# A fourth ring buffer and a third set of gated activations in the loop over expert_v

## The chip, the core and the metric

The kernel runs on one core of one Trainium2 chip, in one launch. The metric is the device time of a whole execution in microseconds (us), median of several runs. Before the change it is 3137.03 us, the median of three runs that took from 3127.26 to 3152.71 us.

## The reference, cut to what matters

The program computes two transformer blocks on 512 tokens of 1024 features in float32. The change touches the end of the second block alone, a feed-forward layer of 16384 experts, each a row `u_e` of `expert_u` and a row `v_e` of `expert_v`:

```python
expert_idx, gates = ...      # 8 heads x 16 experts of every token, with softmax gates
u = jnp.take(expert_u, ib, axis=0)
act = jax.nn.gelu(jnp.einsum('td,thkd->thk', xb, u))
w = gb * act
v = jnp.take(expert_v, ib, axis=0)
out = jnp.einsum('thk,thkd->td', w, v)
```

The layer's output is added to its input, and a last normalisation follows.

## The kernel before

**Tokens.** The 512 tokens are four tiles of 128. For three of them (the dense tiles, `NDENSE = 3`) the kernel computes every expert and multiplies by a gate matrix that is zero for experts not chosen. The fourth tile gathers the 128 chosen rows of each token: 128 indirect DMAs from `expert_u` (here `eu`) and then 128 from `expert_v` (`ev`), each of 128 rows of 1024 floats (512 KB), into a ring of four buffers `urow` (L1323). VectorE works on each gathered tile with one operation: L1332 for `eu` (a product with the token's row, summed), L1342 for `ev` (added to `po`). The gathers are issued by GpSimd (L1324).

**Exact products.** TensorE multiplies in three passes (`mm3`, L261): every operand is split into a high part `hi` and the rest `lo`. A weight tile is 128 x 1024 floats, 512 KB. `_load` (L227) brings it into one of three `raw` buffers by a DMA on SP's queue; `_split` (L232) makes `hi` on ScalarE (L238) and `lo = raw - hi` (L241) on VectorE where the tile's running number is even, on GpSimd where it is odd. `hi` and `lo` have three buffers each. `next_w` (L247), called when tile i is about to be used, sees to it that tiles up to i+2 are split and tiles up to i+4 are being loaded.

**The stage of the change.** `peer` (L1416) first computes 40 of the 128 blocks of activations (`expert_act`, products with `expert_u`, tile name `ut` in DMAs), and the gate matrix, which goes to DRAM (`gd`). Then comes a loop over 128 blocks j of `expert_v` (L1444). Each iteration
- reads, every fourth time, gates of four blocks back (`gread`, two buffers of 768 KB, L1447, on SP's queue);
- gates the activations (`expert_gate`, L1395): `wf` on VectorE (L1400), `wh` on ScalarE (L1403), `wl` on VectorE (L1404), two buffers of each;
- multiplies them by the tile of `expert_v` (`expert_out`, L1407): 18 matmuls of 512 columns into the banks A, B, C and D;
- while j + 40 < 128, computes the activations of block j + 40: 24 matmuls of 384 columns into the bank `acc`;
- issues the gathers of the fourth tile that are due, 2 * 256 / 210 = 2.44 of them in an iteration that also has activations, 1.22 in one that has not (L1469).

In this loop tiles of `ev` and `ut` alternate in the ring for the first 88 iterations; the `ut` tiles are even (`lo` on VectorE), the `ev` tiles odd (`lo` on GpSimd). In the last 40 iterations only `ev` tiles are left and the two engines take turns.

**Order.** Every engine, and SP's queue, works through its instructions in one fixed order. A planner writes that order when the program is built, from the order in which the source names the operations, its own estimate of durations, and the buffers that it believes free; splits are given priority. What is late on the chip holds up everything behind it on the same engine. Each gather is also ordered behind the last GpSimd split that the source has named before it (L1326).

Of the kernel before, what the change touches and what calls it, by code (L numbers as in the profile page):

```python
# [23 lines left out]
# ---------------------------------------------------------------- host layout  # L24
def fm_tiles(w, cols=None):
    """[K, N] -> one [128, (K/128)*128] block per 128 output columns, split into ring tiles of 1024."""
    w = w if cols is None else w[:, cols]
    k, n = w.shape
    a = w.reshape(k // 128, 128, n // 128, 128).transpose(2, 1, 0, 3)
    return a.reshape(n // 128, 128, k // 1024, 1024).transpose(0, 2, 1, 3).reshape(-1, 128, 1024)  # L30


def tm_tiles(w):
    """[K, N] -> ring tiles of [128, 2 k-chunks, 512 columns], column blocks outermost."""
    k, n = w.shape
    a = w.reshape(k // 256, 2, 128, n // 512, 512).transpose(3, 0, 2, 1, 4)
    return a.reshape(-1, 128, 1024)


def fmvec(v):  # L40
# [4 lines left out]
NDENSE = 3      # token tiles whose experts are all computed; the last tile gathers its experts' rows  # L45
NFIFO = 40
IN_ORDER = ((0, 0), (0, 1), (0, 2), (0, 3), (1, 0), (1, 1), (1, 2), (1, 3))      # projections: mixer, heads
ONEHOT = "DDPDDDPP"     # engine of the second one-hot, by quartet of a block
NEARLY, NLATE, NLAG = 25, 3, 10      # products with expert_u before and after the gate matrix
# [3 lines left out]
    [x for n in range(8) for x in [(1, n), (0, n + GATE_AHEAD)] if x[1] < 8]    # gate a, branch; block  # L53
ATTN_STEP = 2
ELEM_AT = 2
FB = "acc; A m fpt; B fs; C pe fpo0; D fpo1"      # banks of the mixers' products
# [33 lines left out]
def prep(inp):  # L90
    """Lays the inputs out; every array is a permutation, slice or stack of inputs, or depends on shapes alone."""
# [77 lines left out]
# ---------------------------------------------------------------- program  # L169
class Prog:  # L170
    def __init__(self, tc, es, I, dbg=None):
        self.tc, self.nc, self.I, self.dbg = tc, tc.nc, I, dbg or {}
        nc = self.nc
        pool = lambda n, b, **k: es.enter_context(tc.tile_pool(name=n, bufs=b, **k))
        self.cp = pool("const", 1)
        self.tp = pool("tiny", 1)
        self.rp = pool("ring", 1)
        self.R = {}
        self.queue = []
        self.qi = 0  # L180
        self.loaded = []
        self.split_done = []
        self.pool_split = None

    # storage: every name of a tile stands for a tag with its number of buffers in the pool of the phase
    def open(self, es, name, spec, right=True, psum=False):
        """spec: "tag buffers name name ...; ..." """
# [9 lines left out]
    def banks(self, spec):  # L197
        """spec: "bank name name; ..." """
# [24 lines left out]
    # ring of weight tiles  # L223
    def want(self, aps):
        self.queue.extend(aps)

    def _load(self):  # L227
        raw = self.rp.tile([128, 1024], F32, tag="raw", name="raw", bufs=3)
        self.nc.sync.dma_start(raw, self.queue[len(self.loaded)])
        self.loaded.append(raw)  # L230

    def _split(self):  # L232
        i = len(self.split_done)
        raw = self.loaded[i]
        hi = self.rp.tile([128, 1024], F32R, tag="hi", name="hi", bufs=3)
        lo = self.rp.tile([128, 1024], F32R, tag="lo", name="lo", bufs=3)
# [10 lines left out]
    def next_w(self):  # L247
        i = self.qi
        self.qi += 1
        while len(self.split_done) < min(i + 3, len(self.queue)):  # L250
# [3 lines left out]
        while len(self.loaded) < min(i + 5, len(self.queue)):  # L254
# [5 lines left out]
    # products  # L260
    def mm3(self, out, a, b, start, stop):  # L261
        """out += a^T b with a, b given as exact (hi, lo) parts"""
# [5 lines left out]
    def gemm_fm(self, X, M=128, bank="acc", parts=1):  # L268
        """one block of 128 output features x 512 tokens; X: list of (hi, lo) FM chunks"""
# [12 lines left out]
    def gemm_tm(self, X, banks=("A", "A", "B", "B"), done=None, tail=2, head=1, ps=None, stop=True, hold=0):  # L282
        """512 output columns x 4 token tiles; the tiles end one after the other,
        the end of a tile behind the norm of the one `hold` before it"""
# [27 lines left out]
    def split(self, src, name):  # L312
        """FM f32 chunk in SBUF -> exact parts"""
# [8 lines left out]
    # constants  # L322
    def consts(self):
# [13 lines left out]
        # derived per-channel vectors  # L337
# [13 lines left out]
        # lower bound: softmax over the two rows, first row  # L351
# [8 lines left out]
        # f = lb + (1 - lb) (tanh / 2 + 1/2) = tanh * c1 + c0  # L360
# [7 lines left out]
    def attn_consts(self):  # L368
        """constants of the first mixers only"""
# [18 lines left out]
    def first_loads(self):  # L388
        """tokens, the first gain and the first weights in the order of their use"""
# [29 lines left out]
    def rstd_of(self, ss, n, eps, w=1):  # L419
        """(ss / n + eps) ** -0.5 of a small tile"""  # L420
# [7 lines left out]
    def new_U(self):  # L428
        """8 FM chunks of exact parts"""
# [4 lines left out]
    def rstd_row(self, ss):  # L434
        """(sum + eps) ** -0.5 of the two scaled square sums of a row"""
# [6 lines left out]
    def square(self, x, ss):  # L442
        """sum of squares / D along the row"""
# [3 lines left out]
    def norm_tile(self, i, gb, banks=("C", "D"), ss=None):  # L447
        """rmsnorm of one token tile of self.X, into its columns of the FM chunks; ss: with its first square sum"""
# [24 lines left out]
    def norm_fm(self, gb):  # L473
        """rmsnorm of self.X as 8 FM chunks of exact parts"""
# [6 lines left out]
    def tm_norm(self, X, gp, gn, early=None):  # L481
        """self.X += rmsnorm(X^T w) * gp, and the FM chunks of rmsnorm(self.X) * gn;
        early: the two halves of the product begun with the first chunks"""
# [35 lines left out]
    # ------------------------------------------------------------ block 1  # L519
# [10 lines left out]
    def lat_part(self, U):  # L530
# [19 lines left out]
        # forget gates of the attention heads: rows 32..39  # L550
# [18 lines left out]
    def fox_proj(self, c, U):  # L569
        """queries, keys and values of two heads"""  # L570
# [84 lines left out]
    def rwkv_elem(self, c):  # L655
        """two heads of the RWKV group on 128 channels"""
# [5 lines left out]
        # decay  # L662
# [15 lines left out]
        # in-context rate  # L678
# [9 lines left out]
        # normalised key  # L688
# [16 lines left out]
        # gate and bonus  # L705
# [15 lines left out]
    def rwkv_group(self, c, g_, e):  # L721
        """operands of four chunks: with Z = [state; values] of a head and U = (I - N)^-1 A0^T Z,
        y = A1^T Z + B1^T U and the next state is D^T Z + Bu^T U"""
# [8 lines left out]
        ar = self.b("AR", [128, 4, 2, 2, 64])         # chunk, A0 or A1, head, token  # L732
        bk = self.b("BK", [128, 4, 4, 64])
        m1 = self.b("M1", [128, 4, 2, 2, 64])         # chunk, head, y or state
        gm = self.b("GM", [128, 4, 2, 64])            # chunk, B1 or Bu
# [11 lines left out]
        # [b k] scaled to the end of their chunk, tokens on partitions  # L747
# [9 lines left out]
        # rows: even head (b; k), odd head: transposed from (k; b)  # L757
# [4 lines left out]
        # scores  # L762
# [18 lines left out]
        # values, tokens on partitions  # L781
# [9 lines left out]
    def rwkv_inv(self, e, g_, h):  # L791
        """(I - N)^-1 of two chunks by doubling"""
# [36 lines left out]
    def rwkv_fold(self, e, g_):  # L829
        """y and the next state as products with Z alone: [A1 D] + A0 ((I - N)^-1)^T [B1 Bu]"""  # L830
# [15 lines left out]
    def rwkv_scan(self, c, g_, e):  # L846
        """chunks in sequence"""
# [20 lines left out]
        # normalise per head, then features on partitions  # L868
# [44 lines left out]
    # ------------------------------------------------------------ block 2  # L913
    def column_sum(self, bank, a, names=("R", "sq")):
        """sums over the partitions, on all of them"""
# [9 lines left out]
    def head_scale(self, sq, n):  # L925
        """(mean square + eps) ** -0.5 of one head on all partitions; sq: sum of n blocks of squares"""
# [16 lines left out]
    def hgrn_in(self, h, U):  # L943
        """forget gate, key and query of one head"""
# [25 lines left out]
    def hgrn(self, h, a, sg):  # L970
# [14 lines left out]
        # the diagonal: sums over the channels, on all partitions  # L985
# [5 lines left out]
        while n <= 256:  # L991
            if n == 64:
                # the earlier tokens of a block by its later ones
# [59 lines left out]
    def gate_hg(self, U):  # L1053
        """sigmoid(gate_a) * (o_hg @ w_branch_hg), doubled"""
# [23 lines left out]
    def ret(self, h, U):  # L1078
# [19 lines left out]
        # scores, keys on partitions: the columns of the later queries  # L1098
# [56 lines left out]
    def merge(self, U):  # L1155
        """M = (sigmoid(gate_a) y_hg + sigmoid(gate_b) y_ret), m1 holds the doubled first term"""
# [31 lines left out]
    def add_out(self, M, gn):  # L1188
        """self.X += M^T w, and the FM chunks of rmsnorm(self.X) * gn"""
# [17 lines left out]
    def row_of(self, i):  # L1207
        """normalised tokens of tile i, tokens on partitions"""
# [23 lines left out]
    def retrieve(self, H4):  # L1232
        """top 16 sub-keys of every (head, half), then the top 16 of the pairs of every head"""
# [8 lines left out]
        for hp in range(4):  # L1242
# [4 lines left out]
            for c in range(4):  # L1247
# [10 lines left out]
                if c % 2:  # L1258
                    # both lists descend: pair (a, b) can only be chosen if (a + 1) (b + 1) <= 16,
                    # which b < 16 for a < 4 and b < 4 for the others contain  # L1260
# [13 lines left out]
    def decode(self, i, hp, ti, bs, bc):  # L1274
        """sub-key numbers (i, j) and gates of two heads of a token tile, slots (head, k) along the free dimension"""
# [34 lines left out]
    def gather_rows(self, i, row):  # L1310
        """experts of one token tile by their rows"""
# [33 lines left out]
    def slots_T(self, i):  # L1345
        """[slot, (i, j, gate), token] of one token tile"""
# [9 lines left out]
    def gate_matrix(self, slT, gd):  # L1356
        """gates[i, j, token] of the dense tokens into DRAM, 32 tokens at a time"""
# [25 lines left out]
    def expert_act(self, H4, j):  # L1383
        """gelu(u . h) of the 128 experts (., j) for the dense tokens"""
# [10 lines left out]
    def expert_gate(self, j, a, gr):  # L1395
        """gated activations of the 128 experts (., j), exact parts"""
        nc = self.nc
        n = NDENSE * 128
        wf = self.C([128, n], "wf", 2)
        nc.vector.tensor_tensor(wf.rearrange("p (b t) -> p b t", t=32), a.rearrange("p (b t) -> p b t", t=32),  # L1400
                                gr[:, :, j % 4, :], op=ALU.mult)
        wh, wl = self.C([128, n], "wh", 2, F32R), self.C([128, n], "wl", 2, F32R)
# [4 lines left out]
    def expert_out(self, ops, acc, i):  # L1407
        """token tile i += its gated activations times their rows of expert_v"""
# [7 lines left out]
    def peer(self, H4, gd, xd, row, out):  # L1416
# [24 lines left out]
        self.open_v()  # L1441
        acc = [[self.b(n) for n in ns] for ns in ("AA", "BB", "CD")]
# [38 lines left out]
    def final(self, i, y, gb, out):  # L1481
        """rmsnorm(self.X + y) of a token tile"""
# [15 lines left out]
def step(gen, n):  # L1498
    """n steps of a generator"""
# [7 lines left out]
def run_all(gens):  # L1507
    """interleave generators round-robin"""
# [9 lines left out]
def body(tc, I, out, dbg=None, manual=False):  # L1518
    nc = tc.nc
    with ExitStack() as es:  # L1520
# [20 lines left out]
        with ExitStack() as e1:  # L1541
# [22 lines left out]
            with ExitStack() as e2:  # L1564
# [3 lines left out]
                def prepare(u):  # L1568
                    """operands of the u-th group of four chunks"""
# [101 lines left out]
```

## Time and profile before

| | |
|---|---|
| median of three runs | 3137.03 us (3127.26 to 3152.71) |
| profiled execution, span from first to last instruction | 3129.2 us (the page gives no other time of it) |
| TensorE busy (matmuls) | 2961.4 us, 95% |
| VectorE, ScalarE, GpSimd busy | 62%, 39%, 48% |
| mean granted TensorE clock | 0.983 |
| the loop over `expert_v`, first matmul to last | 2182.3 to 3121.0 us |

Times below are in microseconds from the span's start. PE is TensorE, DVE is VectorE, ACT is ScalarE, POOL is GpSimd, SPq is SP's queue; PEld is the loading of weights into TensorE. A row such as `lo<-raw,hi` names the tile written and the tiles read. A bracket at the end of a row tells how long the engine had been idle before it and what ended that.

### The profile page before, as it was taken

The numbers are of one execution on the slowest core, as the hardware profiler recorded it, in microseconds if no ns is written. First come the engines' busy times: TensorE is split into PE (matmuls) and PEld (weight loads), VectorE is DVE, ScalarE is ACT, GpSimd is POOL, SyncE is SP. The second block draws the span as 40 slices with busy tenths as digits, with TensorE's granted clock in tenths as the row PEclk, the third lists the DMA queues.
The fourth block names the chain that finished last, engine by engine and source line by source line (L and its number), as shares of the span: only waits on it lengthen the run. The fifth ranks groups of instructions, "written<-read, shape, count | busy, mean of one in ns | idle before, by whom it ended". The sixth has DMA issues, their size and how long they took to land.

```text
span 3129.2 us, 40869 instructions
## 1 busy us (share of the span) xinstructions
PE 2961.4 (95%) x15129; PEld 2547.7 (81%) x15129; DVE 1938.7 (62%) x3421; ACT 1228.4 (39%) x1925; POOL 1508.5 (48%) x1150
## 2 busy tenths in 40 slices
PE   7999898999999999999999978888999999999998
PEld 6877787888878878888888868887888888888876
DVE  4247755443135653555423899997777777787788
ACT  5455644222243433444423324565333333333333
POOL 3222213222245652333323457866767677667665
PEclk9998999999999999999999989999999999999999
DMA  4120013333332213222333223446888988888886
GB/s 156 56 68 8 1 38 109 97 98 97 95 113 69 62 47 101 85 85 85 90 116 123 92 68 95 142 169 219 297 275 293 308 289 298 299 280 299 285 310 240
DMA packets 174359, 473.65 MB, mean 151 GB/s; under 512 B 15056, under 2 KB 64592, under 8 KB 172624
## 3 DMA queue, kind: packets, MB, share of 16 engines
q1 hardware_dynamic: 137296, 336.80, 33.8%
q0 software_dynamic: 36864, 134.23, 12.2%
q8 instruction: 120, 1.97, 0.3%
q14 instruction: 79, 0.65, 0.1%
HBM read 439.49 MB, written 31.46 MB: 151 GB/s over the span
## 4 chain that ended last, share of the span: by engine, by line
PE 69%; DVE 15%; DMA 7%; issue 5%; ACT 2%; POOL 1%; SPq 0%; DVEq 0%; POOLq 0%; ACTq 0%
PE acc L266 13%; PE acc L265 13%; PE acc L264 13%; DMA urow<-ev,ei 3%; PE A L266 3%; PE A L264 3%; PE A L265 3%; PE B L266 3%; PE B L265 3%; PE B L264 3%; DMA urow<-eu,ei 2%; PE pg L1377 2%; DVE lo L241 2%; PE i L804 1%; PE lev L981 1%
## 5 line engine op out<-in xcount | busy, mean ns | idle before, releaser
L241 POOL TENSOR_TENSOR lo<-raw,hi 128x1024 fp32r<-128x1024 f32 x278 | 689.6, 2481 | 912.9 <-ACT hi L238 875.8
L238 ACT ACTIVATE hi<-raw 128x1024 fp32r<-128x1024 f32 x501 | 529.3, 1057 | 1065.7 <-PE acc L265 441.4
L266 PE MATMUL acc<-u,lo 128*128 128x512 f32 (+3 forms) x2344 | 864.6, 369 | 39.2 <-DVE lo L241 21.2
L264 PE MATMUL acc<-u,hi 128*128 128x512 f32 (+3 forms) x2344 | 862.4, 369 | 15.0 <-ACT x L1392 6.3
L265 PE MATMUL acc<-u,hi 128*128 128x512 f32 (+3 forms) x2344 | 862.1, 368 | 0.7 <-DVE u L471 0.7
L266 PEld LDWEIGHTS acc<-u,lo 128*128 128x128 f32 (+1 forms) x2344 | 448.1, 191 | 96.2 <-DVE lo L241 27.6
L264 PEld LDWEIGHTS acc<-u,hi 128*128 128x128 f32 (+1 forms) x2344 | 447.8, 191 | 70.0 <-ACT eact L1392 6.7
L265 PEld LDWEIGHTS acc<-u,hi 128*128 128x128 f32 (+1 forms) x2344 | 448.3, 191 | 54.8 <-issue 2.7
L241 DVE TENSOR_TENSOR lo<-raw,hi 128x1024 fp32r<-128x1024 f32 x223 | 304.4, 1365 | 301.1 <-ACT hi L238 299.9
L1332 DVE SCALAR_TENSOR_TENSOR urow<-urow,h4row 128x1024 f32<-128x1024 f32 x128 | 201.5, 1595 | 109.2 <-DMA urow<-eu,ei 108.9
L1342 DVE SCALAR_TENSOR_TENSOR po<-urow,act,po 128x1024 f32<-128x1024 f32 x127 | 203.2, 1600 | 84.9 <-DMA urow<-ev,ei 83.5
L1324 POOL DMA_INDIRECT urow<-eu,ei x128 | 193.5, 1512 | 32.6 <-issue 19.0
L1324 POOL DMA_INDIRECT urow<-ev,ei x128 | 176.6, 1380 | 37.8 <-issue 18.2
L1403 ACT ACTIVATE wh<-wf 128x384 fp32r<-128x384 f32 x128 | 67.1, 525 | 272.3 <-PE D L265 243.5
L1368 DVE TENSOR_SCALAR ohA<-iota,slT 128x128 f32<-128x128 f32 x384 | 129.8, 404 | 0.9 <-PE pg L1377 0.7
L1377 PE MATMUL pg<-ohB,ohA 128*128 128x128 f32 x768 | 106.3, 280 | 25.0 <-DVE ohB L1374 12.5
L1377 PEld LDWEIGHTS pg<-ohB,ohA 128*128 128x128 f32 x768 | 97.4, 191 | 32.7 <-ACT gstage L1379 16.1
L1379 ACT ACTIVATE gstage<-pg 128x512 f32<-128x512 f32 x96 | 99.5, 1089 | 57.8 <-PE pg L1377 57.7
L1372 POOL TENSOR_SCALAR ohB<-iota,slT 128x128 f32<-128x128 f32 x144 | 98.2, 698 | 39.9 <-PE pg L1377 39.7
L266 PE MATMUL A<-hi,wl 128*128 128x512 f32 x256 | 95.8, 399 | 10.0 <-DVE wl L1404 9.9
L265 PE MATMUL A<-lo,wh 128*128 128x512 f32 x256 | 101.0, 395 | 0.8 <-POOL lo L241 0.8
L264 PE MATMUL A<-hi,wh 128*128 128x512 f32 x256 | 99.8, 390 | 0.6 <-ACT wh L1403 0.6
(539 smaller groups left out, 5395.9 us busy)
## 6 DMA issues: line engine op xcount, KB each, us to landing
raw<-ut SPq DMA_DIRECT2D x128, 512.0 KB
raw<-ev SPq DMA_DIRECT2D x128, 512.0 KB
raw<-w_ret SPq DMA_DIRECT2D x48, 512.0 KB
gd<-gstage SPq DMA_DIRECT2D x12, 2048.0 KB
gread<-gd SPq DMA_DIRECT2D x32, 768.0 KB
raw<-w_gu SPq DMA_DIRECT2D x44, 512.0 KB
raw<-w_hg SPq DMA_DIRECT2D x32, 512.0 KB
raw<-w_in SPq DMA_DIRECT2D x27, 512.0 KB
```

The source lines that it names most:

```text
L238: self.nc.scalar.activation(hi, raw, AF.Copy)
L241: r = eng.tensor_tensor(lo, raw, hi.bitcast(F32), op=ALU.subtract)
L264: mm(out, a[0], b[0], start=start, stop=False)
L265: mm(out, a[0], b[1], start=False, stop=False)
L266: return mm(out, a[1], b[0], start=False, stop=stop).ins
L1324: r = nc.gpsimd.indirect_dma_start(out=u, out_offset=None, in_=src, in_offset=bass.IndirectOffsetOnAxis(ap=ei[:, s:s + 1], axis=0))
L1332: nc.vector.scalar_tensor_tensor(u, u, 1.0, row, op0=ALU.mult, op1=ALU.mult, accum_out=act[:, s:s + 1])
L1342: nc.vector.scalar_tensor_tensor(o, u, act[:, s:s + 1], o, op0=ALU.mult, op1=ALU.add)
L1368: nc.vector.tensor_scalar(A4[:, r], self.iota, sl[:, 0, k + r:k + r + 1], sl[:, 2, k + r:k + r + 1], op0=ALU.is_equal, op1=ALU.mult)
L1372: nc.gpsimd.tensor_scalar(B4[:, r], self.iota, sl[:, 1, k + r:k + r + 1], None, op0=ALU.is_equal)
L1377: last = nc.tensor.matmul(p[:, r, :], A4[:, r], B4[:, r], start=True, stop=True)
L1379: nc.scalar.activation(st[:, :, q * 4:q * 4 + 4].rearrange("p j t -> p t j"), p, AF.Copy)
```

## The change

After the loop's pool has been opened, a flag `ext` is set to 1. From there on tiles whose running number is 3 modulo 4 take their `raw`, `hi` and `lo` from three extra buffers in the loop's pool, so that the ring has four places in place of three; `next_w` splits up to tile i+3 and loads up to tile i+6. `wf`, `wh` and `wl` get three buffers in place of two. No operation is added or taken out. The rest of the diff takes out comments and docstrings.

```diff
@@ __init__
         self.split_done = []
+        self.ext = 0
@@ ring of weight tiles
+    def ring(self, i, name, dt=F32):
+
+        if self.ext and i % 4 == 3:
+            return self.C([128, 1024], name + "x", 1, dt)
+        return self.rp.tile([128, 1024], dt, tag=name, name=name, bufs=3)
+
     def _load(self):
-        raw = self.rp.tile([128, 1024], F32, tag="raw", name="raw", bufs=3)
-        self.nc.sync.dma_start(raw, self.queue[len(self.loaded)])
+        i = len(self.loaded)
+        raw = self.ring(i, "raw")
+        self.nc.sync.dma_start(raw, self.queue[i])
         self.loaded.append(raw)
@@ _split
-        hi = self.rp.tile([128, 1024], F32R, tag="hi", name="hi", bufs=3)
-        lo = self.rp.tile([128, 1024], F32R, tag="lo", name="lo", bufs=3)
+        hi, lo = self.ring(i, "hi", F32R), self.ring(i, "lo", F32R)
@@ next_w
-        while len(self.split_done) < min(i + 3, len(self.queue)):
+        while len(self.split_done) < min(i + 3 + self.ext, len(self.queue)):
...
-        while len(self.loaded) < min(i + 5, len(self.queue)):
+        while len(self.loaded) < min(i + 5 + 2 * self.ext, len(self.queue)):
@@ expert_gate
-        wf = self.C([128, n], "wf", 2)
+        wf = self.C([128, n], "wf", 3)
...
-        wh, wl = self.C([128, n], "wh", 2, F32R), self.C([128, n], "wl", 2, F32R)
+        wh, wl = self.C([128, n], "wh", 3, F32R), self.C([128, n], "wl", 3, F32R)
@@ peer
         self.open_v()
+        self.ext = 1
```

## Rows read from the trace of the kernel before

**Rows 1.** Stretches: length, busy of PE, PEld, DVE, ACT, POOL; clock, DMA share, GB/s.
```profile
2182.20:2941.00 758.80, 737.44 (x3672) 665.75 (x3673) 571.71 (x609) 255.73 (x353) 536.30 (x301) 0.99 0.87 292
2941.00:3121.00 180.00, 168.88 (x722) 135.16 (x720) 153.66 (x151) 62.16 (x91) 110.26 (x63) 0.99 0.83 283
```
**Rows 2.** Timeline of TensorE: start, duration. Ends of the two stretches, one iteration between.
```profile
2182.26 0.50 PE L264 MATMUL A<-hi,wh 128*128 128x512 f32 x1 [0.31 <-ACT wh L1403]
...
2336.20 0.39 PE L264 MATMUL A<-hi,wh 128*128 128x512 f32 x1
...
2340.32 0.33 PE L264 MATMUL acc<-u,hi 128*128 128x384 f32 x1
...
2344.51 0.39 PE L264 MATMUL A<-hi,wh 128*128 128x512 f32 x1
...
2941.07 0.39 PE L264 MATMUL A<-hi,wh 128*128 128x512 f32 x1
...
3120.62 0.39 PE L266 MATMUL D<-hi,wl 128*128 128x512 f32 x1
```
**Rows 3.** Groups of TensorE's instructions from 2182.2 to 2941.0: count, busy, mean ns.
```profile
L266 PE MATMUL acc<-u,lo 128*128 128x384 f32 x696 | 238.0, 342 | 21.3 <-DVE lo L241 21.2
```
**Rows 4.** TensorE's waits from 2182.2 to 2941.0: total us, times, longest.
```profile
PE acc L266 <- DVE lo L241: 21.2, 19, 4.2
```
**Rows 5.** TensorE's waits from 2941 to 3121.
```profile
PE A L266 <- DVE wl L1404: 9.9, 7, 4.2
```
**Rows 6.** A short stretch (columns of rows 1) with the clock at half.
```profile
2312.00:2318.00 6.00, 4.79 (x15) 4.79 (x16) 5.97 (x10) 0.00 (x0) 3.34 (x3) 0.50 0.79 218
```
**Rows 7.** Timelines of three engines around one short wait of TensorE.
```profile
2349.03 1.05 ACT L238 ACTIVATE hi<-raw 128x1024 fp32r<-128x1024 f32 x1
...
2352.23 1.23 DVE L1332 SCALAR_TENSOR_TENSOR urow<-urow,h4row 128x1024 f32<-128x1024 f32 x1 [1.31 <-DMA urow<-eu,ei]
...
2354.44 3.43 DVE L241 TENSOR_TENSOR lo<-raw,hi 128x1024 fp32r<-128x1024 f32 x1
...
2357.92 0.44 PE L266 MATMUL acc<-u,lo 128*128 128x384 f32 x1 [0.48 <-DVE lo L241]
```
**Rows 8.** VectorE's waits from 2200 to 2930 (columns of rows 4).
```profile
DVE urow L1332 <- DMA urow<-eu,ei: 105.6, 59, 3.7
```
**Rows 9.** Tile urow from 2180 to 3110: ns min/median/max, first and last start; landing.
```profile
L1324 POOL DMA_INDIRECT urow<-eu,ei x128: 937/1682/2007, 2181.4 to 2632.4; - x128
...
L1342 DVE SCALAR_TENSOR_TENSOR po<-urow,act,po x127: 1271/1285/3370, 2646.5 to 3103.9; 128x1024 f32<-128x1024 f32 x127
...
DMA to landing us min/median/max: 4.2/6.5/9.6
```
**Rows 10.** Timelines of VectorE and GpSimd in the last stretch.
```profile
2984.17 4.03 POOL L241 TENSOR_TENSOR lo<-raw,hi 128x1024 fp32r<-128x1024 f32 x1 [1.63 <-ACT hi L238]
...
2985.97 2.64 DVE L1400 TENSOR_TENSOR wf<-eact,gread 128x384 f32<-128x384 f32 x1
2988.53 2.59 DVE L1342 SCALAR_TENSOR_TENSOR po<-urow,act,po 128x1024 f32<-128x1024 f32 x2
...
2989.74 0.95 POOL L1324 DMA_INDIRECT urow<-ev,ei  x1 [0.30 <-issue]
```
**Rows 11.** Durations of splits and gating in the whole loop (columns of rows 9).
```profile
L241 DVE TENSOR_TENSOR lo<-raw,hi x107: 1208/1219/3426, 2184.1 to 3112.3; 128x1024 fp32r<-128x1024 f32 x107
L241 POOL TENSOR_TENSOR lo<-raw,hi x106: 2352/2407/4253, 2188.1 to 3105.7; 128x1024 fp32r<-128x1024 f32 x106
...
L1400 DVE TENSOR_TENSOR wf<-eact,gread x96: 546/558/3155, 2236.1 to 3078.2; 128x384 f32<-128x384 f32 x96
```
**Rows 12.** Waits of ScalarE and of SP's queue in the loop.
```profile
ACT wh L1403 <- PE D L265: 243.5, 100, 4.1
...
SPq L1447 <- DVE wf L1400: 117.5, 29, 8.4
```
**Rows 13.** A short stretch (columns of rows 1) with DMA engines full.
```profile
2834.00:2838.00 4.00, 4.00 (x21) 3.49 (x21) 2.21 (x3) 1.44 (x2) 0.34 (x1) 1.00 0.99 352
```

## The prediction

> **What bounds the kernel now.** I read the loop over `expert_v` alone, because nothing outside it changes: first the busy time by stretch, then TensorE's timeline and its waits, then the engines that it waits for.
>
> By stretch [rows 1], TensorE is busy 737.4 of 758.8 us in the 88 iterations that also compute activations, and 168.9 of 180.0 in the last 40. The timeline gives the price of an undisturbed tile [rows 2]: the matmuls of a tile of `expert_v` start at 2336.20, those of the next `expert_u` tile at 2340.32, the next `expert_v` tile at 2344.51. So 4.12 us and 4.19 us, together 8.31 us. The first stretch, 2182.26 to 2941.07, holds 87 `expert_u` tiles (696 low-part matmuls, 8 a tile [rows 3]) and so 88 of `expert_v`: 88 x 4.12 + 87 x 4.19 = 727.1 us. It takes 758.8, an excess of 31.7 us. The last stretch should take 40 x 4.12 = 164.8 and takes 179.9 (to 3121.0, the last start plus 0.39): an excess of 15.1 us. **The change can return 46.8 us at most**, 1.5% of the kernel; no tile gets cheaper by it.
>
> The excess of the first stretch has a name: 19 waits for VectorE's `lo`, 21.2 us, the longest 4.2 [rows 4]. Behind the longest the granted clock stands at 0.50 of full speed, the 1.2 GHz level, in all of the 6 us shown [rows 6]: TensorE had stood idle before it fell. Such stretches, and gaps too small for the waits view, make up the other 10.5 us. One ordinary wait shows how it comes about [rows 7]: `hi` of the tile starts at 2349.03 and takes 1.05, so that `lo` could start at 2350.1. But VectorE stands in its fixed order before gathered rows that have not landed (1.31 us idle just before 2352.23), and starts `lo` at 2354.44; TensorE needed it 0.48 us before it came. In that stretch VectorE waits 105.6 us for gathers of `expert_u` alone [rows 8].
>
> **The change, part by part.** Nothing is added to or removed from any engine's work: the same loads, splits, gatings, gathers and matmuls. What moves is how early a tile may be split and loaded.
>
> *The fourth hi and lo.* In steady state `hi` of tile i+2 waits until tile i-1 has left its buffers; now it is tile i+3 that takes that place. The split starts at the same moment as before and is needed one tile later, 4.12 to 4.19 us. Every wait in rows 4 is at most 4.2 us, so one tile of margin covers each taken singly. They return only if lateness carries over from one iteration to the next. VectorE's room against that: 571.7 us busy in 758.8 [rows 1], 6.5 us of an iteration's 8.31, and most of its idle time is waiting for gathers, which passes when it runs late, since the rows have then landed. I take 28 of the 31.7 us (all but about a tenth), bounds 0 (order and lateness move along with the tile) and 31.7.
>
> *The fourth raw.* A load is issued when the place frees, so the same number of bytes goes out, with one tile more in flight. SP's queue is fixed too: loads stand behind `gread`, which waited 117.5 us in 29 times for the last `wf` of its buffer [rows 12]; a load held there now has a tile more before its split is late. Queue time added: none. DMA at full TensorE pace: an iteration moves two tiles of 512 KB, a quarter of 768 KB and 2.44 gathers of 512 KB, 2464 KB or 2.52 MB, in 8.31 us: 304 GB/s against 292 now at a share of 0.87 [rows 1]. In the last 40 it is 512 + 192 + 624 KB, 1.36 MB in 4.12 us: 330. A short stretch with the DMA engines full moved 352 [rows 13]. So the first stretch fits and the last one barely; cost 0 in the first, included below in the last.
>
> *The third gating set.* ScalarE stood 243.5 us before `wh` until TensorE had released the older set [rows 12], with the next `hi` queued behind it. That wait moves back by a tile; next in line there is the ring's own release, so alone it gives little in the first stretch. In the last it aims at the 9.9 us for `wl` [rows 5], where TensorE's waits lie.
>
> *The last 40.* What is late next is visible there. While GpSimd's `lo` ran, VectorE's `wf` took 2.64 us instead of 0.56 and GpSimd's `lo` 4.03 instead of 2.41 [rows 10, 11]: the two take turns. One tile then needs 1.22 x 1.285 for rows [rows 9], about 0.56 each for `wf` and `wl`, half of 1.22 and half of 2.41 for `lo` [rows 11]: 1.57 + 1.12 + 0.61 + 1.20 = 4.50 us. Consecutive rows of VectorE overlap a little (the `wf` of rows 10 ends at 2988.61, 0.08 us after the next operation started), and 3.7 such ends a tile bring it to 4.2. That is no less than TensorE's 4.12, and the stretch now goes at 179.9 / 40 = 4.50. A ring does not shorten this turn-taking, it only fills its gaps. I take 5 of the 15.1 us, bounds 0 and 15.1, nearer the lower, since the engine pair already needs the tile's time.
>
> The Trainium skill (SBUF — State Buffer, the box on VectorE blocking DMA) says more: while VectorE runs an operation that takes both port pairs, GpSimd cannot write the descriptors of its own DMAs. If the row sums were of that kind, the gathers' issue would join the turn-taking, 1.22 x 0.95 us a tile or more, and the last stretch could return nothing: a sum of 28. The rows do not bear that out: an issue of 0.95 us, among the shortest, ran inside a pair of unstretched `po` operations [rows 9, 10].
>
> *Start of the loop.* The new buffers lie in the loop's pool, so the first use may wait for memory of the gate phase. Tiles already loaded keep their old `raw`; the first `wf` waits for that phase anyway. I take 0, bounds 0 and 4 us (one tile).
>
> **The sum.** 28 + 5 = 33 us. The profiled span is 3129.2; it would become 3096. The median of the runs is 7.8 above that span, so I set the sum against the median: 3137 - 33 = **3104 us**, -1.05%.
>
> **Rivals.** *The whole excess goes* (chance 0.08): the pair of engines closes its gaps too, 3137 - 46.8 = 3090. For it: the waits for `wl` are exactly what the third set is for. Against: the 4.2 us above.
>
> *The wait moves along* (0.22): the planner puts each split just as far back in VectorE's order as it now has margin, or bandwidth at 304 GB/s makes the gathers land later, and half or less of the first stretch comes back: gain 0 to 17, time 3120 to 3137, middle 3128. For it: splits here run at planned places and VectorE does wait on gathers all along. Against: splits have priority, and nothing is put between.
>
> *Gathers become the bound* (0.12), the case on the slower side. The ring `urow` keeps four buffers. A gather holds one for about 1.7 us of issue, 6.5 of flight and 1.2 of VectorE, 9.4; four gathers come every 4 x (2632.4 - 2181.4) / 127 = 14.2 us [rows 9], so 4.8 us are free. A gather is ordered behind the last split GpSimd was given before it in the source; that split is now of a tile further ahead, which can hold the issue by up to a tile, 4.15 us, and one more 512 KB load in flight takes 1.8 us at 292 GB/s. Together 5.95, that is 1.1 over the free time; from 4.8 on each us over costs 256 / 4 = 64 us, so up to 3137 + 70 = 3207, and 3172 at half the overrun. Against: the ordering shifts the phase rather than the rate, and the longest landing, 9.6, is 3.1 above the median.
>
> That the change doesn't act is unlikely, since the numbers modulo 4 rotate through four places; if the planner loaded no earlier, the time stays 3137 (in the second rival).
>
> **How the numbers follow.** About 1% (31 us) is what a measurement of this kernel tells from no change. The forecast's own case has 0.58: 3095 to 3115, so a little over half of it lies below 3105.7. Faster: 0.33 + 0.08 + 0.02 = 0.43. Same: 0.25 + 0.20 = 0.45. Slower: 0.12. The range runs from 3086 (full excess, with a few us for the runs' spread) to 3140, which takes in the second rival and leaves out most of the third.
>
> **What would show it.** Right: in the first stretch the waits for `lo` fall below about 3 us, no half-clock stretch is left, an iteration takes 8.31 nearly throughout, and DMA rises to about 304 GB/s; the last 40 still take near 4.4 us each with the pair of engines full. Wrong: waits for `lo` of the same count and size at other places; TensorE waiting for `raw`; gathers landing well over 6.5 us, with GpSimd waiting for `urow`; or a last stretch near 165 us, which would refute the turn-taking bound.

## The result, and the profile after

The changed kernel takes **3087.99 us**, the median of four runs (3084.94 to 3091.29), against 3135.9 for the kernel before, run beside it (3127.26 to 3152.71). The ratio is 0.986, 95% interval 0.9829 to 0.9892. That is 48 us less; the forecast was 33 less and 3104 us, the range 3086 to 3140.

The profiled executions differ by 45.2 us in span, 3129.2 to 3084.0. Busy time of the two stretches of the loop after, with the columns of [rows 1]:

```profile
2177.00:2905.60 728.60, 728.60 (x3684) 663.12 (x3683) 570.02 (x607) 258.09 (x353) 535.70 (x300) 1.00 0.88 304
2905.60:3076.00 170.40, 165.31 (x722) 134.56 (x720) 159.39 (x152) 60.62 (x89) 110.77 (x65) 1.00 0.84 300
```

TensorE is busy all of the first stretch, the clock is granted whole, and the DMA engines move the 304 GB/s that the forecast asked of them, at a share of 0.88. VectorE and GpSimd do the same work as before, 570.0 and 535.7 us busy against 571.7 and 536.3, in 30 us less. TensorE's timeline, start and duration, at the bounds of the stretches (they answer to [rows 2]):

```profile
2177.41 0.39 PE L271 MATMUL A<-hi,wh 128*128 128x512 f32 x1
...
2905.66 0.39 PE L271 MATMUL A<-hi,wh 128*128 128x512 f32 x1
...
3075.43 0.39 PE L273 MATMUL D<-hi,wl 128*128 128x512 f32 x1
```

The first stretch takes 728.25 us in place of 758.8, within 1.2 us of the 727.1 reckoned for undisturbed tiles. The last takes 170.2 (to 3075.8) in place of 179.9. So the loop returns 30.6 + 9.8 = 40.4 us. The other 4.85 us lie ahead of it: the loop begins at 2177.41 in place of 2182.26, although the instructions stand in the same order in both programs up to some 8 us ahead of the loop. I take that part for drift between two executions: with only the gating sets changed, the kernel before began its loop at 2178.2.

TensorE's waits in the loop after (engine, line, what it waited for: total us, times, longest), one row where [rows 4, 5] had waits of 21.2 and 9.9:

```profile
PE A L273 <- DVE wl L1411: 4.9, 6, 1.9
```

The 19 waits for VectorE's `lo` are gone, with the half-clock stretches behind them. What has not gone is VectorE's waiting for gathered rows (from 2190 to 2905, the same columns), beside [rows 8]:

```profile
DVE urow L1339 <- DMA urow<-eu,ei: 91.5, 56, 5.0
DVE po L1349 <- DMA urow<-ev,ei: 56.2, 36, 4.8
```

By the median the gathers land no sooner (tile `urow`, min/median/max, beside the last row of [rows 9]):

```profile
DMA to landing us min/median/max: 2.0/7.0/10.8
```

VectorE still stands before late rows, up to 5.0 us at a time. TensorE no longer notices. The margin shows why. From the end of a `lo` on VectorE to the first matmul that reads it, the trace of before has a median of 3.6 us, and for 21 of the 87 `expert_u` tiles under 0.3. After the change the median is 7.4 us and the shortest 1.9: nearly one tile's time more. The planner's order of VectorE changed as well (every `lo` of the first stretch stood right behind a `wf`, now 25 of 85 do); what that does apart from the margin was not tried.

### The profile page after: what moved, and what is told of

It reads as the page before. It is cut to its first block, busy times and chain, and to the rows that moved or that the text cites. A ratio compares the mean times of both kernels' runs of the same rounds, so it can differ in the third digit from the quotient of the medians.

```text
span 3084.0 us, 40810 instructions
## 1 busy us (share of the span) xinstructions
PE 2945.5 (96%) x15129; PEld 2542.2 (82%) x15129; DVE 1940.8 (63%) x3421; ACT 1229.7 (40%) x1925; POOL 1507.6 (49%) x1150
## 4 chain that ended last, share of the span: by engine, by line
PE 77%; DVE 13%; issue 4%; DMA 2%; ACT 2%; POOL 2%; SPq 0%; DVEq 0%; POOLq 0%; ACTq 0%
PE acc L272 14%; PE acc L271 14%; PE acc L273 14%; PE A L273 3%; PE A L272 3%; PE A L271 3%; PE B L272 3%; PE B L271 3%; PE B L273 3%; PE pg L1384 2%; DMA urow<-ev,ei 2%; PE i L811 2%; PE lev L988 1%; DVE wk L1235 1%; PE C L273 1%
## 5 line engine op out<-in xcount | busy, mean ns | idle before, releaser
L248 POOL TENSOR_TENSOR lo<-raw,hi 128x1024 fp32r<-128x1024 f32 x224 | 553.0, 2470 | 758.2 <-ACT hi L245 729.1
L245 ACT ACTIVATE hi<-raw 128x1024 fp32r<-128x1024 f32 x447 | 472.5, 1057 | 944.2 <-PE acc L272 496.2
L248 DVE TENSOR_TENSOR lo<-raw,hi 128x1024 fp32r<-128x1024 f32 x223 | 318.2, 1427 | 297.3 <-ACT hi L245 297.0
L1349 DVE SCALAR_TENSOR_TENSOR po<-urow,act,po 128x1024 f32<-128x1024 f32 x127 | 193.9, 1527 | 66.4 <-DMA urow<-ev,ei 65.6
L1410 ACT ACTIVATE wh<-wf 128x384 fp32r<-128x384 f32 x128 | 67.2, 526 | 313.8 <-PE D L272 268.7
L248 POOL TENSOR_TENSOR lox<-rawx,hix 128x1024 fp32r<-128x1024 f32 x53 | 137.9, 2602 | 97.8 <-ACT hix L245 97.6
L1411 DVE TENSOR_TENSOR wl<-wf,wh 128x384 fp32r<-128x384 f32 x128 | 101.4, 794 | 5.8 <-ACT wh L1410 4.1
L1407 DVE TENSOR_TENSOR wf<-eact,gread 128x384 f32<-128x384 f32 x98 | 69.0, 705 | 17.3 <-ACT eact L1399 16.2
```

The lines of the kernel that those rows point to most:

```text
L245: self.nc.scalar.activation(hi, raw, AF.Copy)
L248: r = eng.tensor_tensor(lo, raw, hi.bitcast(F32), op=ALU.subtract)
L1349: nc.vector.scalar_tensor_tensor(o, u, act[:, s:s + 1], o, op0=ALU.mult, op1=ALU.add)
L1411: nc.vector.tensor_tensor(wl, wf, wh.bitcast(F32), op=ALU.subtract)
```

## The experiments

### One part at a time

**The ring alone** (two gating sets):

```diff
-        wf = self.C([128, n], "wf", 3)
+        wf = self.C([128, n], "wf", 2)
...
-        wh, wl = self.C([128, n], "wh", 3, F32R), self.C([128, n], "wl", 3, F32R)
+        wh, wl = self.C([128, n], "wh", 2, F32R), self.C([128, n], "wl", 2, F32R)
```

> The changed kernel with two sets of wf, wh and wl again: the fourth place of the ring alone. Theory 1 (a split needs one tile of margin against VectorE standing before gathered rows that have not landed): the first stretch of the loop stays near its undisturbed time, 728 to 732 us against 758.8 before, no waits for lo; the last 40 iterations lie between 170 (changed) and 180 (before). Total 3088 to 3098 us. Theory 2 (the third gating set does it, since ScalarE no longer stands before wh with the next hi behind it): the waits for lo are back, total above 3120.

Measured: 3088.09 us, ratio 0.9859 (0.9836 to 0.9882), the same as the whole change. TensorE's waits in its loop:

```profile
PE A L273 <- DVE wl L1411: 2.7, 6, 1.0
PE acc L271 <- ACT eact L1399: 1.1, 1, 1.1
```

The first stretch takes 728.4 us and the last 169.8. The ring is the whole gain.

**The gating sets alone** (the kernel before with three sets):

```diff
-        wf = self.C([128, n], "wf", 2)
+        wf = self.C([128, n], "wf", 3)
...
-        wh, wl = self.C([128, n], "wh", 2, F32R), self.C([128, n], "wl", 2, F32R)
+        wh, wl = self.C([128, n], "wh", 3, F32R), self.C([128, n], "wl", 3, F32R)
```

> The kernel before with three sets of wf, wh and wl and the ring as it was. Theory 1: the first stretch keeps most of its excess, 750 to 759 us with some 15 to 21 us of waits for lo; the last 40 lose waits for wl and come to 172 to 178. Total 3120 to 3135 us. Theory 2: the first stretch falls to 735 or less, total 3095 to 3105.

Measured: 3142.23 us, ratio 1.0028 (1.0006 to 1.0049): no gain, and by the interval a trifle slower. Theory 2 falls. Theory 1's sizes were missed too: the stretches of the profile take 783.3 and 182.2 us. In the last one the waits for `wl` are gone, as expected, but waits for `lo` (the second row) stand in their place. Waits of TensorE and, in the last row, of ScalarE:

```profile
PE acc L266 <- DVE lo L241: 41.0, 22, 4.6
PE A L265 <- DVE lo L241: 13.7, 6, 6.1
...
ACT wh L1403 <- PE D L265: 197.9, 88, 7.4
```

ScalarE still stands before `wh` for 198 us (243.5 in [rows 12], 268.7 after the change). I take it that the planner uses a third set to gate one block further ahead and then waits for the next release. The order of TensorE is that of the kernel before up to the last 40 iterations, that of VectorE is not, and the profiled execution is 11 us slower than the median of its runs. How much of the 783 us is due to the third set and how much to one slow execution is not told apart. Without margin the same order does spread. The run with the last 40 on VectorE in the kernel before (further below) has on every engine the order of the kernel before, up to the last 12 us of the first stretch, and takes 768.8 us for it against 758.8. The kernel before ran from 3124 to 3158 us in all the comparisons here, the kernels with the full ring and no other edit from 3082 to 3092.

**The fourth raw alone**, one load more ahead, splits no earlier:

```diff
-        hi, lo = self.ring(i, "hi", F32R), self.ring(i, "lo", F32R)
+        hi = self.rp.tile([128, 1024], F32R, tag="hi", name="hi", bufs=3)
+        lo = self.rp.tile([128, 1024], F32R, tag="lo", name="lo", bufs=3)
...
-        while len(self.split_done) < min(i + 3 + self.ext, len(self.queue)):
+        while len(self.split_done) < min(i + 3, len(self.queue)):
...
-        while len(self.loaded) < min(i + 5 + 2 * self.ext, len(self.queue)):
+        while len(self.loaded) < min(i + 5 + self.ext, len(self.queue)):
```

It has two gating sets, as has the next kernel.

> The fourth place for raw alone, one load more ahead; hi and lo, the reach of the split and the gating sets as before. Theory 1: a split is no earlier, so the waits for lo stay; total 3118 to 3136 us. Theory 3 (late loads behind gread on SP's queue are what makes the splits late): most of the gain is here, total 3095 to 3105, and ScalarE's waits for raw fall from 140 us to under 40.

Measured: 3110.77 us, ratio 0.993 (0.991 to 0.995). Waits of TensorE (the long ones) and the longest of ScalarE:

```profile
PE acc L274 <- DVE lo L249: 21.0, 18, 2.3
PE A L274 <- DVE wl L1412: 3.1, 4, 1.2
...
ACT wh L1411 <- PE D L273: 277.8, 108, 2.6
ACT hi L246 <- PE acc L273: 261.7, 85, 6.9
```

ScalarE's waits for raw tiles have fallen to 2.0 us, and still TensorE waits 21.0 us for `lo`, though never over 2.3 at a time, where before it was up to 4.2: first stretch 754.4 us, in the slowest of the four runs. The last stretch has come down to 171.3. Both expectations are half right: half of the gain is here.

**The fourth hi and lo alone**, splits one tile further ahead, three raw buffers:

```diff
-        raw = self.ring(i, "raw")
+        raw = self.rp.tile([128, 1024], F32, tag="raw", name="raw", bufs=3)
...
-        while len(self.loaded) < min(i + 5 + 2 * self.ext, len(self.queue)):
+        while len(self.loaded) < min(i + 5 + self.ext, len(self.queue)):
```

> The fourth place for hi and lo alone, splits one tile further ahead; three raw buffers and two gating sets as before, as many loads waiting as before. Theory 1: the margin comes from here, the first stretch is within 8 us of 728 and the total 3090 to 3105 us. Theory 3: raw still comes late, ScalarE keeps waiting over 100 us for it, and the total stays above 3118.

Measured: 3125.56 us, ratio 0.9972 (0.9954 to 0.999); first stretch 746.6, last 177.9, in the fastest of its ten runs. Waits of TensorE, then of ScalarE:

```profile
PE A L273 <- DVE wl L1411: 7.0, 10, 2.2
PE acc L273 <- DVE lo L248: 6.5, 8, 1.8
...
ACT hi L245 <- DMA raw<-ut: 244.9, 65, 13.7
ACT hi L245 <- DMA raw<-ev: 83.3, 37, 10.0
ACT hix L245 <- DMA raw<-ev: 64.4, 30, 5.2
```

Theory 3 held: now the raw tile is what is late, 393 us of ScalarE's waits. A split may only be one tile earlier if its load is too. Neither part is the gain; raw gives 0.7%, hi and lo 0.3%, both together 1.4%.

### What makes the splits late

**VectorE without its waits for rows.** The kernel before, in which the row operations read the fourth tile's own row: the same work and the same gathers, but no wait for a landing (`junk` is a buffer of its own).

```diff
-            nc.vector.scalar_tensor_tensor(u, u, 1.0, row, op0=ALU.mult, op1=ALU.mult, accum_out=act[:, s:s + 1])
+            nc.vector.scalar_tensor_tensor(junk, row, 1.0, row, op0=ALU.mult, op1=ALU.mult, accum_out=act[:, s:s + 1])
...
-                nc.vector.scalar_tensor_tensor(o, u, act[:, s:s + 1], o, op0=ALU.mult, op1=ALU.add)
+                nc.vector.scalar_tensor_tensor(o, row, act[:, s:s + 1], o, op0=ALU.mult, op1=ALU.add)
```

> The kernel before (three places, two gating sets) with every gather issued as before, but VectorE's row operations reading the fourth tile's own row in place of the gathered one: the same work and the same bytes, no standing before rows that have not landed; the result of the fourth token tile is left out by it. Theory 1 (that standing makes the splits late): waits for lo nearly vanish with three places, the first stretch is 728 to 736 us, the total 3095 to 3110. Theory 3 (raw comes late whatever VectorE does): 745 us or more, total 3118 or more, with ScalarE waiting over 100 us for raw.

Measured: 3169.11 us, ratio 1.0101 (1.006 to 1.0142), slower than the kernel before. By its numbers this meets theory 3: the first stretch takes 815.4 us, and ScalarE waits 151 us for raw tiles (`ev` and `ut`). But it does not isolate the waits for rows, because freed of the gathers the planner moved the row operations far ahead, and VectorE's order is another one. Waits of TensorE, of VectorE and of ScalarE:

```profile
PE acc L266 <- DVE lo L241: 60.4, 34, 3.5
...
DVE wl L1405 <- ACT wh L1404: 274.3, 67, 7.6
...
ACT hi L238 <- DMA raw<-ev: 131.2, 26, 9.5
```

VectorE now stands before `wh` instead of before rows, and `lo` is late all the same: it can be late with no wait for rows at all.

**The same with the order nearer to that of the kernel before**: each row operation is held behind its gather in the planner's order, with no wait on the chip (the diff is against the run just told).

```diff
+            self.rd = r.ins
             return u
+
+        def behind(x):
+            self.tc.add_manual_dep(x.ins, self.rd.name,
+                                   mybir.DependencyInfo(mybir.DependencyClass.NoSync, mybir.DependencyReason.DATA),
+                                   reason="row work stays behind its gather in the plan")
...
-                nc.vector.scalar_tensor_tensor(o, row, act[:, s:s + 1], o, op0=ALU.mult, op1=ALU.add)
+                behind(nc.vector.scalar_tensor_tensor(o, row, act[:, s:s + 1], o, op0=ALU.mult, op1=ALU.add))
```

> The kernel before with VectorE's row operations reading the fourth tile's own row in place of the gathered one, as in the run without row waits, but each now held behind its gather in the planner's order (with no wait on the chip), so that VectorE's order stays close to that of the kernel before; the result of the fourth token tile is left out by it. Theory 1 (standing before rows that have not landed makes lo late): with three places the waits for lo nearly vanish, the first stretch is 728 to 738 us, the total 3090 to 3112. Theory 3 (late raw tiles make it whatever VectorE does): ScalarE waits over 100 us for raw and the first stretch stays at 745 or more, total 3115 or more.

Measured: 3083.51 us, ratio 0.9832 (0.9803 to 0.986), with three places and two gating sets: better than either expectation. A stretch of its first part (columns of [rows 1]), then waits of TensorE and of ScalarE:

```profile
2180.00:2900.00 720.00, 720.00 (x3639) 655.15 (x3638) 512.93 (x604) 254.15 (x348) 501.87 (x298) 1.00 0.89 305
```
```profile
PE A L265 <- DVE lo L241: 2.2, 3, 0.7
PE A L266 <- DVE wl L1411: 0.9, 3, 0.3
...
ACT hi L238 <- DMA raw<-ut: 10.5, 9, 2.1
ACT hi L238 <- DMA raw<-ev: 9.9, 5, 3.4
```

TensorE never stops in 720 us, and raw tiles are no longer late either (20 us of waits, where the kernel before had 140 for `ev` alone). So the late loads follow from a late VectorE: a late `lo` frees its `raw` late, and SP's queue issues the next load late.

What makes VectorE late this run does not settle, because its edit changed two things more. In 37 of 85 cases VectorE's `lo` now stands ahead of a `wf` that stood ahead of it before. And no `lo` of VectorE is drawn out any more; I call an operation drawn out where it takes longer than its like because GpSimd's `lo` runs beside it. Durations of VectorE's `lo` in the first stretch (columns of [rows 9]), in the kernel before and in this run:

```profile
L241 DVE TENSOR_TENSOR lo<-raw,hi x88: 1208/1219/3426, 2184.1 to 2940.3; 128x1024 fp32r<-128x1024 f32 x88
```
```profile
L241 DVE TENSOR_TENSOR lo<-raw,hi x88: 1211/1220/1229, 2181.0 to 2901.3; 128x1024 fp32r<-128x1024 f32 x88
```

Ten of the 88 in the kernel before took 3.4 us in place of 1.22, and behind each of the ten TensorE stood idle, for 0.1 to 0.5 us. These are its shortest waits, 3 us in all. Ahead of the longest, the 4.2 us of [rows 4], stands a raw tile that landed late (ScalarE, start and duration):

```profile
2307.46 1.06 ACT L238 ACTIVATE hi<-raw 128x1024 fp32r<-128x1024 f32 x1 [5.79 <-DMA raw<-ev]
```

So VectorE is late both from standing before rows that have not landed and from being drawn out, and the runs here do not divide the lateness between the two. What they show is that with both away from its `lo` three places are enough, and that a full place more for raw, hi and lo lets both stand without harm: in the changed kernel a `lo` of VectorE still takes up to 3.43 us, with no wait behind it.

### What is left in the last 40 iterations

**The changed kernel with `lo` of the last 40 tiles on one engine**, VectorE (0) or GpSimd (1):

```diff
             pool = i % 2 if self.pool_split is None else self.pool_split
+            if i >= len(self.queue) - 40:
+                pool = 0
```

> The changed kernel, but lo of the last 40 weight tiles always on VectorE. Turn-taking theory (in the last 40 iterations VectorE and GpSimd's lo exclude each other, some 4.2 us a tile): without GpSimd's lo a tile needs 1.57 + 1.12 + 1.22 = 3.9 us less overlaps, under TensorE's 4.12, so the stretch falls from 170.2 to 165 to 167 us and the total by 3 to 5 us, to about 3083 to 3085. Rival (the 330 GB/s that the stretch asks of the DMA engines, or late gathers, hold it): it stays at 169 to 172 us and the total at 3088.

> The changed kernel, but lo of the last 40 weight tiles always on GpSimd. Turn-taking theory: a tile needs 1.57 + 1.12 + 2.41 = 5.1 us less overlaps of about 0.25, 4.8: the stretch comes to 188 to 196 us, the total to 3106 to 3114. If GpSimd alone were the limit (2.41 of lo and 1.22 issues of 1.35 plus gaps of 0.3): 4.4 a tile, 177 us, total 3095. DMA rival: 169 to 172, total 3088.

Measured: 3081.4 us on VectorE (ratio 0.9825, 0.9794 to 0.9856), 3112.93 on GpSimd (0.992, 0.9895 to 0.9945). The last stretch by busy time (columns of [rows 1]), VectorE first:

```profile
2906.60:3070.00 163.40, 163.19 (x720) 134.81 (x718) 143.19 (x170) 61.36 (x90) 56.09 (x45) 1.00 0.86 310
```
```profile
2909.50:3104.00 194.50, 173.85 (x721) 136.75 (x720) 190.74 (x132) 60.20 (x88) 152.66 (x84) 0.97 0.75 262
```

163.4 us, below the 165 to 167 expected, is the undisturbed stretch: 4.085 us a tile, a little less than the 4.12 that I had taken from iterations with activations. With `lo` on GpSimd it takes 194.8, inside the 188 to 196 of the turn-taking theory and outside GpSimd's own 177, and VectorE shows as busy for 98% of it, since its operations are drawn out while GpSimd's run. With `lo` on VectorE, the DMA engines give 310 GB/s at a share of 0.86, so they were not the limit. In the changed kernel an operation drawn out in this way looks so (VectorE, then GpSimd, start and duration):

```profile
2947.16 2.75 DVE L1411 TENSOR_TENSOR wl<-wf,wh 128x384 fp32r<-128x384 f32 x1
```
```profile
2946.18 3.31 POOL L248 TENSOR_TENSOR lo<-raw,hi 128x1024 fp32r<-128x1024 f32 x1 [0.64 <-ACT hi L245]
```

GpSimd's `lo` waits for VectorE's rows until about 2947, and VectorE's `wl`, 0.55 us otherwise, until it ends at 2949.5.

**The kernel before with the last 40 on VectorE** (the same two lines, three places):

> The kernel before (three places) with lo of the last 40 weight tiles always on VectorE. If turn-taking made the excess of 15 us in its last stretch, it falls to 164 to 168 and the total by 12 to 15 us, to about 3122. If late raw tiles made most of it (the run with four raw places alone brought the stretch to 171), it stays at 172 to 180 and the total falls by 0 to 7 us, to 3129 to 3136.

Measured: 3122.46 us, ratio 0.9956 (0.9933 to 0.998). The stretch falls to 163.4 without any place more (columns of [rows 1]):

```profile
2951.30:3115.00 163.70, 163.32 (x721) 134.87 (x719) 141.90 (x171) 63.22 (x91) 64.43 (x43) 1.00 0.86 310
```

So the last stretch's whole excess, 16.5 us over 163.4, goes when GpSimd's splits go; a place more for raw takes off 8.6 of it by closing gaps. But the splits make the excess only together with VectorE's rows. Two runs from above keep half of the splits on GpSimd, with three places: the run without row waits, whose planner had put all rows ahead of this stretch, and the run with planned rows, which has them in it but waits for no landing (columns of [rows 1], in this order):

```profile
2998.40:3162.50 164.10, 163.73 (x722) 134.89 (x720) 70.59 (x106) 60.99 (x91) 91.61 (x63) 1.00 0.88 311
```
```profile
2903.90:3072.20 168.30, 165.20 (x721) 134.47 (x719) 154.29 (x147) 61.41 (x91) 106.06 (x63) 1.00 0.87 303
```

Without rows the splits cost 0.7 us; with rows that are never late, 4.9. The rest of the 16.5 went with the waits for rows. One thing rides along in both kernels with `lo` on VectorE: no new GpSimd split stands in the last 40 iterations, so their gathers are no longer ordered behind one. The two runs just shown keep that order, so by itself it costs little where VectorE does not wait for the rows; with late rows it was not tried apart.

**Both, with two gating sets**:

> The fourth place of the ring alone (two gating sets) with lo of the last 40 tiles always on VectorE. If the third gating set gives nothing in either stretch, this equals the run with three sets and lo on VectorE, about 3083 to 3085 us; if the set is needed once VectorE does more in the last stretch, waits for wl return there and it is 2 to 6 us slower than that.

Measured: **3079.33 us**, ratio 0.982 (0.9789 to 0.985), below the 3083 to 3085 expected, equal to the run with three sets and lower than either kernel. TensorE takes 728.2 and 163.4 us for the stretches and has no wait in the loop that the waits view lists; the loop holds nothing more for buffers to return.

**Three buffers for gathered rows** in the changed kernel:

```diff
-            u = self.C([128, D], "urow", 4)
+            u = self.C([128, D], "urow", 3)
```

(the same number stands in two other places of the loop's end)

> The changed kernel with three buffers for the gathered rows in place of four. If the ring of rows is as near its limit as my slower rival had it: a gather holds its buffer 9.85 us in the changed kernel, about 0.7 more pass before the buffer is used again, 10.5 in all, against 3 x 3.41 = 10.2 that three buffers allow at this pace; each us over costs 256 / 3 = 85 us, so 15 to 35 us more than the changed kernel, 3103 to 3123. If the time that a gather holds its buffer shrinks with fewer in flight, 0 to 10 us more, 3088 to 3098.

Measured: 3100.03 us, ratio 0.9897 (0.9859 to 0.9935), 12 us over the changed kernel, just under the first theory's 15 to 35 and over the second's 10. Waits of GpSimd for a buffer of rows, then TensorE's:

```profile
POOL urow L1331 <- DVE po L1349: 111.3, 85, 3.5
POOL urow L1331 <- DVE urow L1339: 90.3, 77, 2.9
```
```profile
PE A L273 <- DVE wl L1411: 12.6, 10, 4.8
```

GpSimd waits 202 us for buffers, against 25 with four, but the first stretch stays at 728.2; all of the loss is in the last, 182.0 us. The ring of rows is near its limit only where the pair of engines is full as well.

## Why the prediction was right, and where its terms were off

**What can be returned** held. The forecast allowed 46.8 us and the loop returned 40.4 in the profile. The medians differ by 48, because the 4.85 us ahead of the loop and some 3 us between the profiled executions and the medians come on top.

**The fourth hi and lo** were priced at 28 us for the first stretch, which returned 30.6; the carrying over of lateness that I had kept as a bound did not happen. Of the reason, VectorE before its rows, the forecast saw one half. In the wait that it read, [rows 7], `lo` not only starts late but then takes 3.43 us in place of 1.22, because GpSimd's `lo` runs beside it:

```profile
2354.03 2.75 POOL L241 TENSOR_TENSOR lo<-raw,hi 128x1024 fp32r<-128x1024 f32 x1 [2.31 <-ACT hi L238]
```

At 1.22 us it would have been there some 1.7 us before TensorE needed it, as late as it started. The taking of turns, which the forecast priced for the last 40 alone, is at work in the first stretch too. The term also stood under the wrong heading. I had put the gain on hi and lo and "cost 0" on raw, and took every load for timely because its queue had one tile more. Hi and lo alone returned 12.2 us of that stretch in their one profile, raw alone 4.4, both 30.6; with a stretch that drifts by 10 us between executions of one order these two sizes are rough, and the medians put raw ahead. ScalarE's 140 us of waits for raw tiles stood in the trace of before, and the sum left them out:

```profile
ACT hi L238 <- DMA raw<-ev: 140.3, 35, 10.1
```

**The third gating set** was to give little in the first stretch, which is right, and to aim at the 9.9 us for `wl` in the last, which is wrong: with two sets the last stretch is as short (169.8 and 170.2 us). `wl` was late because VectorE was, not for want of a buffer: with three sets and the ring as it was, `lo` was late in its place.

**The last 40** is the term that was mis-sized: 5 us forecast, 9.8 measured. The mechanism, the taking of turns, was right and is shown both ways, by 163.4 us without GpSimd's `lo` and 194.8 with all of it there. My own floor of 4.2 us a tile would have allowed 179.9 - 168 = 12. I took less than half of that, because I did not believe that a deeper ring could close the pair's gaps. It did, nearly all of them: the stretch runs at 170.2 / 40 = 4.25 us a tile, at that floor.

**The Trainium skill's rule** that GpSimd cannot write descriptors while VectorE runs an operation on both port pairs (SBUF — State Buffer, the box on VectorE blocking DMA) would have kept the last stretch from falling at all, if VectorE's operations here were of that kind. The trace does not show them to be. With `lo` on VectorE, VectorE was busy 143.2 of 163.4 us, and GpSimd's issues took 55.4:

```profile
L1333 POOL DMA_INDIRECT urow<-ev,ei x43 | 55.4, 1289 | 70.9 <-DVE po L1351 59.3 <-DMA urow<-ev,ei 10.4 <-issue 1.2
```

That is 199 us together in 163.4, so for 35 us at least they ran side by side. The row, gating and split operations of this kernel take turns with GpSimd's `lo`; no run here shows that they do so with its issues.

**The rivals.** That the wait moves along did not come true in either stretch. That the whole excess goes did in the first alone. Gathers as the bound did not come true with four buffers: landing rose only from 6.5 to 7.0 us, and GpSimd's waits for a buffer only from 13.7 to 25.0 us in all. Its price was too high too. With three buffers the first stretch lost nothing, where 85 us for each us over would have shown at once: with three a gather held its buffer for 9.35 us on average, with four for 9.85.

**The sum** of 33 us was low by the 4.8 us of the last 40, the 2.6 of the first stretch and some 5 to 8 us outside the loop or between executions, which no step of it was about.

## What to carry to other kernels

An engine that stands, in its fixed order, before a transfer that has not landed, or whose operations another engine draws out, makes everything behind it late, including loads whose buffers it frees. Here the bottleneck engine's waits were each no longer than about one tile's time, and one more place in the whole chain (raw and split together) hid them; a place in one link alone left waits at the next link. Where two causes make an engine late, taking one away can shift the other: look at the durations of its operations too, not only at its waits. Before adding buffers, add up the time of operations that cannot run side by side: where that sum exceeds the bottleneck's time a tile, moving work between the two engines returns what buffers can't.

## What was not expected of the hardware

GpSimd's `lo` takes 2.41 us and VectorE's 1.22 for the same tile, and while GpSimd's runs, an operation of VectorE with two inputs is drawn out by nearly all of the overlap (`wl` 2.75 in place of 0.55). So giving GpSimd half of the splits made the last stretch 6.8 us longer than leaving all of them to VectorE. An engine's busy share in a profile then counts the wait for the other engine as work: 98% for VectorE in a stretch where its own work is 55% by the undrawn durations (1.57 + 1.12 = 2.69 of 4.87 us a tile).
